# A two-layer hybrid block: instructions ordered by the scheduler's simulated timeline

## The chip, the cores and the metric

The program runs on one core of one Trainium2 chip. A core has a matrix engine (PE), a vector engine (DVE), a scalar engine (ACT), a general engine (POOL) and a queue engine (SP) that here only issues transfers. The engines share on-chip memory, run side by side and meet at semaphores. The metric is the device time of one execution in microseconds.

## What is computed

The reference is a backbone of two layers over 512 latent tokens and 256 context tokens, 1024 wide. One layer is, with the branches cut to their names:

```
h  = rmsnorm(x, g) * (1 + scale) + shift            # adaLN, scale/shift/gate from c
q, k, v, za, xr, zr, us, zs, gates = split(h @ w_in)
ya = diff_attention(q, k, v)    # 4 heads, two softmaxes each, head norm
yr = rglru(conv4(xr))           # both directions, block-diagonal gates
ys = glu(s5(us))                # both directions, complex diagonal states
m  = sum_n sigmoid(gates_n) * ((y_n * silu(z_n)) @ w_branch_n)
x  = x + gate * (m @ w_out)
```

Context tokens read context tokens only; latent tokens read all. The second layer needs no context output. A last norm gives the latent tokens.

## The kernel before

Tokens lie along the free axis, 512 latent and then 256 context, and channels on the 128 partitions. Each large product is three fp32r products (high by high, low by high, high by low), written by `product` (L180): per block of 128 input channels and per segment of tokens a 128x512 matmul and, where context is needed, a 128x256 one. `inproj` makes one tile `ps_in` of 128 output channels so, in 48 such matmuls (24 without context); `branch` makes `ps_b` in 24 (12). `wsplit` brings weights: SP loads `wr` (L161), ACT copies it to the high half `wh` (L162), and DVE forms the low half `wl` (L167); in a part of layer 0 a POOL transfer does instead.

A layer is written in this order. First the input of the S5 branch (`ps_us`). Then four LRUs, `lru(i)`: `ps_in`, a convolution on ACT and DVE (L822 to L827, tile `cv`), the split `uHL` (L830), four gate products `ps_g` of six matmuls each with an ACT function behind each (L840), then exponentials, a square root (L853) and three scans on DVE (L855, L858, L856, and a sum at L859). All tiles of the pool `lru` have one buffer: `cv` shares the place of `th`, which the sum at L859 reads last, and `uHL` that of `a2`. Between the LRUs stand the sixteen steps of the S5 scan (`ps_x`, `ps_y`), as many as a table `PLAN` says, and gate projections. Then come the LRU's output path, the S5's, and attention.

Attention (L1065 to L1118) goes head by head. For each block of 128 queries and each of two components, `ps_s` is a score block of four matmuls over 768 keys (two over 256 keys for the context queries); DVE takes its maximum (L1089, L1090) and ACT its exponential with the sum (L1091). The two components are put together on DVE (L1094 to L1097), transposed on PE (`ps_t`), split, and multiplied by the values (`ps_o`, L1113). After each head stand two output chunks of the S5 branch, each a gate projection `ps_in` and a `ps_b`. After the fourth head the squares of all heads are summed (`ps_ss`, L1128), a root is taken, and `ps_rr` (L1136) spreads it, one head at a time, to DVE (L1137).

The accumulator memory sets the pace: pool `acc` has two buffers of 1024 columns, `mis` two of 512 (`ps_t`, `ps_o`, `ps_x`, `ps_y`), and `big` **one** of 1024. `big` holds `ps_s`, `ps_g`, `ps_ss`, `ps_rr` in layer 0 and the queries' `ps_in` of every second head. So a score block starts only when ACT has read the block before. In layer 1 `big` becomes part of another pool after the LRUs.

The order of the instructions on each engine is not written by hand. The program text gives each instruction a place, which is its priority; a scheduler then walks through an imagined execution and, whenever an engine is free in it, issues the first instruction in program order whose operands and buffers are ready there. Each engine then keeps that order on the chip. Products of a later part of the program thus fill the gaps of a chain in an earlier part; they are called fill below. What counts as ready, and at which moment an engine is free, follows from the time that the scheduler has for each instruction.

## Time and profile before

| what | us |
|---|---|
| median of 3 runs | 1568.6 (1568.36 to 1571.8) |
| the profiled execution | 1571.89, of which the span is 1570.1 |
| PE busy with matmuls | 1489.2 (95%) |
| DVE busy | 1125.0 (72%) |
| ACT busy | 818.7 (52%) |
| POOL busy | 172.2 (11%) |

The profiled execution took 3.3 us more than the median. Times in the stretches named later count from the start of the span. The stages lie so in it: load, norm and S5 input of layer 0 up to 72 us; its LRUs and S5 scan to 355; S5 output and start of attention to 440; heads 0 and 1 to 574, heads 2 and 3 with the head norm to 720; merge, output projection and next norm to 935; S5 input of layer 1 to 990; its LRUs and S5 scan to 1137; outputs to 1250; attention to 1465; and the rest.

### The profile page before, as it was taken

What the parts mean: (1) busy time and instruction counts of PE and PEld (TensorE: products, weight loads), DVE (VectorE), ACT (ScalarE), POOL (GpSimd) and SP (SyncE); (2) the same over time, 40 slices, a digit from 0 to 9 for tenths busy, and PEclk for the clock granted to TensorE, in tenths of its full rate; (3) what the DMA queues carried; (4) which work ended last, traced back from release to release, by engine and by line L of the source; (5) the groups of instructions that cost most, each with busy time, mean ns of one, the idle gap of its engine ahead of it and who ended that gap; (6) DMA issues with size and microseconds to landing.
All of it is one profiled execution on the core that took longest, in us unless ns stands there. A gap on an engine that the chain in (4) does not pass through costs nothing. (4 is left out here: it accounts for less than half of the span.)

```text
span 1570.1 us, 24750 instructions
## 1 busy us (share of the span) xinstructions
PE 1489.2 (95%) x9096; PEld 1246.2 (79%) x9096; DVE 1125.0 (72%) x2312; ACT 818.7 (52%) x1468; POOL 172.2 (11%) x231
## 2 busy tenths in 40 slices
PE   4998899899999999999999999999999999999997
PEld 2786778788988888888778887777788988888777
DVE  6789899978367757658568863789775488397555
ACT  6676878664344534534325365666525365355433
POOL 1111111124000100000332310000000000000110
PEclk8998999999999999989999999999999999999999
DMA  8555444467311111115573762435454212111542
GB/s 279 167 151 119 112 110 105 89 158 197 94 52 43 42 53 46 49 34 177 193 250 125 258 201 82 143 111 162 118 168 132 81 61 58 65 61 54 174 148 94
DMA packets 111210, 189.13 MB, mean 120 GB/s; under 512 B 25328, under 2 KB 42352, under 8 KB 111088
## 3 DMA queue, kind: packets, MB, share of 16 engines
q1 hardware_dynamic: 97392, 158.17, 32.2%
q0 software_dynamic: 13696, 29.37, 8.1%
q8 instruction: 72, 1.18, 0.3%
q14 instruction: 50, 0.41, 0.1%
HBM read 145.02 MB, written 25.69 MB: 109 GB/s over the span
## 5 line engine op out<-in xcount | busy, mean ns | idle before, releaser
L162 ACT ACTIVATE wh<-wr 128x512 fp32r<-128x512 f32 x320 | 200.3, 629 | 367.2 <-PE ps_in L180 151.3
L180 PE MATMUL ps_in<-hH,wh 128*128 128x512 f32 x1248 | 376.5, 360 | 14.4 <-ACT wh L162 7.3
L180 PE MATMUL ps_in<-hH,wl 128*128 128x512 f32 x1248 | 378.6, 359 | 7.1 <-DMA wl<-wr 7.1
L180 PE MATMUL ps_in<-hL,wh 128*128 128x512 f32 x1248 | 375.5, 359 | 0.0
L167 DVE TENSOR_TENSOR wl<-wr,wh 128x512 fp32r<-128x512 f32 x264 | 187.5, 714 | 172.7 <-ACT wh L162 129.9
L180 PEld LDWEIGHTS ps_in<-hH,wh 128*128 128x128 f32 x1248 | 207.3, 192 | 52.3 <-ACT wh L162 8.4
L180 PEld LDWEIGHTS ps_in<-hH,wl 128*128 128x128 f32 x1248 | 207.7, 191 | 43.1 <-DMA wl<-wr 9.6
L180 PEld LDWEIGHTS ps_in<-hL,wh 128*128 128x128 f32 x1248 | 206.9, 191 | 31.8
L911 POOL TENSOR_TENSOR m<-m,g 128x768 f32<-128x768 f32 (+1 forms) x16 | 29.0, 1811 | 730.7 <-issue 348.4
L1091 ACT ACTIVATE p<-ps_s,mx 128x768 f32<-128x768 f32 (+1 forms) x80 | 65.2, 815 | 71.4 <-DVE mx L1090 67.5
L180 PE MATMUL ps_b<-yH,wh 128*128 128x512 f32 (+1 forms) x288 | 89.5, 359 | 0.6 <-DVE m L945 0.6
L180 PE MATMUL ps_b<-yL,wh 128*128 128x512 f32 (+1 forms) x288 | 88.0, 357 | 0.0
L180 PE MATMUL ps_b<-yH,wl 128*128 128x512 f32 (+1 forms) x288 | 87.7, 357 | 0.0
L1089 DVE TENSOR_REDUCE mx<-ps_s 128x1 f32<-128x768 f32 (+1 forms) x80 | 67.6, 847 | 23.9 <-PE ps_s L1086 23.3
L165 POOL DMA_DIRECT2D wl<-wr x56 | 49.0, 896 | 259.6 <-ACT wl L164 206.1
L180 PEld LDWEIGHTS ps_b<-yH,wh 128*128 128x128 f32 x288 | 48.2, 188 | 10.7 <-ACT wl L164 0.9
L180 PEld LDWEIGHTS ps_b<-yL,wh 128*128 128x128 f32 x288 | 47.7, 188 | 7.2
L180 PEld LDWEIGHTS ps_b<-yH,wl 128*128 128x128 f32 x288 | 47.6, 188 | 7.2
L180 PE MATMUL acc<-mH,wh 128*128 128x512 f32 (+1 forms) x160 | 49.2, 340 | 0.0
L180 PE MATMUL acc<-mH,wl 128*128 128x512 f32 (+1 forms) x160 | 48.8, 337 | 0.0
L180 PE MATMUL acc<-mL,wh 128*128 128x512 f32 (+1 forms) x160 | 48.8, 337 | 0.0
L1107 DVE TENSOR_TENSOR wTL<-ps_t,wTH 128x512 fp32r<-128x512 f32 (+1 forms) x72 | 35.9, 536 | 13.4 <-ACT wTH L1106 13.2
(357 smaller groups left out, 2901.1 us busy)
## 6 DMA issues: line engine op xcount, KB each, us to landing
wr<-in_win SPq DMA_DIRECT2D x208, 256.0 KB
wm<-in_wmod SPq DMA_DIRECT2D x48, 512.0 KB
wl<-wr POOLq DMA_DIRECT2D x56, 256.0 KB, 3.9
wr<-in_wbr SPq DMA_DIRECT2D x48, 256.0 KB
sp<-s5d SPq DMA_DIRECT2D x16, 768.0 KB
wr<-in_wout SPq DMA_DIRECT2D x32, 256.0 KB
s5d<-vv POOLq DMA_DIRECT2D x16, 320.0 KB, 3.2
usd<-up SPq DMA_DIRECT2D x8, 512.0 KB
```

The costliest lines, as they stand in the source:

```text
L162: S.activation(wh, raw, AF.Copy)
L165: G.dma_start(wl, raw, accum_op=OP.add)
L167: V.tensor_sub(wl, raw, f32(wh))
L180: PE.matmul(out[:, c0:c0 + n], lhsT=(wl if ps == 2 else wh)[:, k, :], rhs=rhs(k0 + k, ps == 1)[:, t0:t0 + n], start=st, stop=en)
L911: (V if n == 0 and dt >= ADD_V[l] else G).tensor_add(m_t[dt][:, :W], m_t[dt][:, :W], g[:, :W])
L1089: V.reduce_max(mx[:, 0:1], sc[:, :kw], axis=AX.X)
L1091: S.activation(p[c][:, :kw], sc[:, :kw], AF.Exp, bias=mx[:, 1:2], scale=0.125, accum_out=sm[:, c:c + 1])
L1107: V.tensor_sub(wTL[:, k0:k1, qi * 128:(qi + 1) * 128], src, f32(wTH[:, k0:k1, qi * 128:(qi + 1) * 128]))
```

## The change

One argument is added where the program is scheduled. The scheduler held a running sum of the durations of what it had issued to each engine, and took that for the time; now a simulation of the machine's timeline runs along with it and says what is done and which engine is free. No instruction of the computation is added or taken away: PE has the same matmuls, DVE, POOL and SP the same work, and ACT two loads of a function table fewer (34 for 36). Only their order on each engine differs, and with it the waits.

```diff
--- before.py
+++ after.py
@@ -1337,7 +1337,7 @@
         arrays[f"in_{name}"] = a[name]
         args.append(nc.dram_tensor(f"in_{name}", a[name].shape, F32, kind="ExternalInput").ap())
     args.append(nc.dram_tensor("out_T", (8, 128, T), F32, kind="ExternalOutput").ap())
-    with tile.TileContext(nc) as tc:
+    with tile.TileContext(nc, schedule_with_timeline_sim=True) as tc:
         hybrid_kernel(tc, *args)
     r = _run(nc, [arrays], core_ids=[0])
     o = np.asarray(r.results[0]["out_T"])
```

On PE the order differs over most of the program; it is alike at about 0 to 60 us, 360 to 440 and 1500 to 1560 us of the span of before. Three places follow. In the rows, a tile's name is followed by a running number.

The first is PE at the end of head 1 in layer 0. `ps_s` are the last score blocks, of context queries; `ps_v` is the values product of heads 2 and 3, and `ps_in_6127` the query projection of head 2, which takes the one buffer of `big`. Before:

```order
L1113 MATMUL ps_o_5663<-wTH_5585,vL_4562 128x256 x6
L1103 MATMUL ps_t_5707<-ident_105,p0_5685 128x128 x2
L1083 MATMUL ps_s_5715<-ks_5479,qs_5406 128x256
L1086 MATMUL ps_s_5715<-kL_4558,qs_5406 128x256
L1014 MATMUL ps_v_5941<-wh_5986,hL_325 128x256 x4
L1014 MATMUL ps_v_5942<-wh_5986,hL_325 128x256 x2
L1014 MATMUL ps_v_5941<-wl_5987,hH_324 128x256 x4
L1014 MATMUL ps_v_5942<-wl_5987,hH_324 128x256 x2
L1014 MATMUL ps_v_5941<-wh_6028,hH_359 128x256 x4
L1083 MATMUL ps_s_5722<-ks_5479,qs_5406 128x256
L1086 MATMUL ps_s_5722<-kL_4558,qs_5406 128x256
L1014 MATMUL ps_v_5942<-wh_6028,hH_359 128x256 x2
```

After:

```order
L1083 MATMUL ps_s_5695<-ks_5479,qs_5406 128x256
L1086 MATMUL ps_s_5695<-kL_4558,qs_5406 128x256
L1113 MATMUL ps_o_5663<-wTH_5585,vH_4561 128x256 x6
L1113 MATMUL ps_o_5663<-wTL_5586,vH_4561 128x256 x6
L1113 MATMUL ps_o_5663<-wTH_5585,vL_4562 128x256 x6
L1083 MATMUL ps_s_5715<-ks_5479,qs_5406 128x256
L1086 MATMUL ps_s_5715<-kL_4558,qs_5406 128x256
L1103 MATMUL ps_t_5707<-ident_105,p0_5685 128x128 x2
L1083 MATMUL ps_s_5722<-ks_5479,qs_5406 128x256
L1086 MATMUL ps_s_5722<-kL_4558,qs_5406 128x256
L180 MATMUL ps_in_6127<-hH_235,wh_6116 128x512
L180 MATMUL ps_in_6127<-hH_235,wh_6116 128x256
```

The rows of `ps_v` have gone from between the score blocks to a place ahead of them, and the query projection follows the last score block at once. The same holds ten score and transpose tiles back: between `ps_s_5539` and `ps_in_6127` no matmul of another part stands in the order of after. The end of head 3 looks alike there, from `ps_s_6977` to the third `ps_rr`.

The second is PE between the third and fourth LRU of layer 1. `ps_g_10982` is the last gate product of the third LRU, `ps_g_11303` the first one of the fourth, and `ps_in` are projections. Before:

```order
L180 MATMUL ps_g_10982<-uHL_10952,wl_10874 128x512
L180 MATMUL ps_g_10982<-uHL_10952,wl_10874 128x256
L180 MATMUL ps_in_11191<-hH_10005,wl_11187 128x512
L180 MATMUL ps_in_11191<-hH_10027,wh_11186 128x512
L180 MATMUL ps_in_11191<-hL_10028,wh_11186 128x512
L180 MATMUL ps_in_11191<-hH_10027,wl_11187 128x512
L180 MATMUL ps_in_11191<-hH_10031,wh_11186 128x512
L180 MATMUL ps_in_11191<-hL_10032,wh_11186 128x512
L180 MATMUL ps_in_11191<-hH_10031,wl_11187 128x512
L180 MATMUL ps_in_11235<-hH_9985,wl_11225 128x512
```

After:

```order
L180 MATMUL ps_g_10982<-uHL_10952,wh_10873 128x512
L180 MATMUL ps_g_10982<-uHL_10952,wh_10873 128x256
L180 MATMUL ps_g_10982<-uHL_10952,wl_10874 128x512
L180 MATMUL ps_g_10982<-uHL_10952,wl_10874 128x256
L180 MATMUL ps_g_11303<-uHL_11297,wh_11218 128x512
L180 MATMUL ps_g_11303<-uHL_11297,wh_11218 128x256
L180 MATMUL ps_g_11303<-uHL_11297,wh_11218 128x512
L180 MATMUL ps_g_11303<-uHL_11297,wh_11218 128x256
L180 MATMUL ps_g_11303<-uHL_11297,wl_11219 128x512
L180 MATMUL ps_g_11303<-uHL_11297,wl_11219 128x256
```

The projections that stood between the two LRUs, 16.33 us of PE's time there, have gone to an earlier place; from `ps_g_10974` to the fourth LRU's last gate product 36 gate matmuls stand in a row.

The third is PE at the norm ahead of layer 1. `ps_st` sums squares, `ps_rb` spreads the root, `ps_us` is the first product of layer 1, and `ps_w` and `acc` are output projections of layer 0. Before:

```order
L180 MATMUL ps_w_9824<-mH_9083,wh_9587 128x512
L215 MATMUL ps_rb_9803<-ident_105,rs_9800 128x128 x2
L180 MATMUL ps_w_9824<-mL_9084,wh_9587 128x512
L180 MATMUL ps_w_9824<-mH_9083,wl_9588 128x512
L180 MATMUL ps_w_9824<-mH_9087,wh_9593 128x512
```

After:

```order
L180 MATMUL acc_9878<-mH_9099,wh_9704 128x512
L207 MATMUL ps_st_9797<-ones_110,norm_0_9778 128x2 x2
L180 MATMUL acc_9878<-mL_9100,wh_9704 128x512
L180 MATMUL acc_9878<-mH_9099,wl_9705 128x512
L215 MATMUL ps_rb_9803<-ident_105,rs_9800 128x128 x2
L180 MATMUL ps_us_10060<-hH_9985,wh_9968 128x256
L180 MATMUL ps_us_10061<-hH_9985,wh_9974 128x256
```

The output projections that stood behind `ps_rb` now stand ahead of it, and the first product of layer 1 follows it directly.

## Rows read from the trace of the kernel before

**Rows 1.** The page: the span, and section 1, busy time, share and instructions.

```profile
span 1570.1 us, 24750 instructions
...
PE 1489.2 (95%) x9096; PEld 1246.2 (79%) x9096; DVE 1125.0 (72%) x2312; ACT 818.7 (52%) x1468; POOL 172.2 (11%) x231
```

**Rows 2.** Stages (us): length, busy (instructions) of PE, PEld, DVE, ACT, POOL; clock, DMA share, GB/s.

```profile
72.00:355.00 283.00, 260.29 (x1809) 218.04 (x1809) 251.56 (x556) 207.31 (x400) 41.79 (x49) 0.97 0.53 124
...
440.00:574.00 134.00, 131.94 (x826) 115.40 (x825) 87.06 (x169) 62.76 (x121) 8.14 (x4) 1.00 0.15 46
574.00:720.00 146.00, 144.25 (x848) 124.48 (x847) 96.34 (x181) 68.85 (x128) 7.37 (x4) 0.96 0.15 46
...
990.00:1137.00 147.00, 136.94 (x794) 111.69 (x791) 127.54 (x257) 91.72 (x122) 0.00 (x0) 0.97 0.43 129
...
1250.00:1465.00 215.00, 212.72 (x1185) 179.61 (x1184) 153.15 (x279) 110.70 (x204) 12.73 (x8) 0.99 0.20 61
```

**Rows 3.** Waits of PE in 72 to 355 us: total us, times, longest.

```profile
PE ps_in L180 <- ACT wh L162: 7.3, 3, 3.7
```

**Rows 4.** Order of time, a full score step: start us, us, engine, line, operation.

```profile
533.50 0.61 PE L1083 MATMUL ps_s<-ks,qs 128*128 128x512 f32 x2
...
534.90 0.95 DVE L1089 TENSOR_REDUCE mx<-ps_s 128x1 f32<-128x768 f32 x1
...
536.13 0.90 ACT L1091 ACTIVATE p<-ps_s,mx 128x768 f32<-128x768 f32 x1 [1.93 <-DVE mx L1090]
...
537.50 0.51 PE L1083 MATMUL ps_s<-ks,qs 128*128 128x512 f32 x2
```

**Rows 5.** Order of time, a context score step of the same head.

```profile
552.50 0.36 PE L1083 MATMUL ps_s<-ks,qs 128*128 128x256 f32 x1
...
554.88 0.39 PE L1083 MATMUL ps_s<-ks,qs 128*128 128x256 f32 x1
```

**Rows 6.** Four stretches, matmuls into ps_in alone; columns as in rows 2.

```profile
526.10:556.50 30.40, 4.65 (x25) 3.75 (x25) 0.00 (x0) 0.80 (x1) 1.00 0.15 45
671.40:718.00 46.60, 26.07 (x120) 20.34 (x121) 1.89 (x2) 1.61 (x2) 0.89 0.13 44
1069.90:1091.90 22.00, 16.33 (x79) 13.11 (x79) 0.00 (x0) 2.03 (x4) 1.00 0.42 130
1444.70:1467.40 22.70, 15.11 (x53) 9.97 (x53) 0.68 (x1) 0.58 (x1) 0.92 0.18 54
```

**Rows 7.** Two of these stretches, matmuls into ps_b alone.

```profile
526.10:556.50 30.40, 5.33 (x24) 3.67 (x24) 0.94 (x1) 1.00 0.15 45
671.40:718.00 46.60, 3.65 (x17) 2.52 (x17) 0.94 (x1) 0.89 0.13 44
```

**Rows 8.** The first of these stretches, matmuls into ps_v alone.

```profile
526.10:556.50 30.40, 11.14 (x87) 10.81 (x88) 0.00 (x0) 0.00 (x0) 1.00 0.15 45
```

**Rows 9.** Order of time, first and third broadcast of the head norms.

```profile
712.23 0.82 PE L1136 MATMUL ps_rr<-ident,rs 128*128 128x128 f32 x6
...
717.07 0.82 PE L1136 MATMUL ps_rr<-ident,rs 128*128 128x128 f32 x6
```

**Rows 10.** Order of time, third LRU of layer 1 to the fourth's input.

```profile
1070.37 0.89 ACT L840 ACTIVATE gi<-ps_g,prm 128x768 f32<-128x768 f32 x1
...
1084.61 0.68 DVE L859 TENSOR_TENSOR ysum<-ysum,th 128x512 f32<-128x512 f32 x1
...
1090.46 0.84 ACT L830 ACTIVATE uHL<-u 128x768 fp32r<-128x768 f32 x1 [0.88 <-DVE u L827]
```

**Rows 11.** Order of time, the norm ahead of layer 1.

```profile
920.43 0.58 PE L207 MATMUL ps_st<-ones,norm 128*128 128x2 f32 x4 [1.35 <-DVE norm L202]
...
922.07 0.42 DVE L225 TENSOR_TENSOR xn<-xn,ps_rb 128x256 f32<-128x256 f32 x1 [0.56 <-PE ps_rb L215]
```

**Rows 12.** Two stretches near the end of layer 0's attention; columns as in rows 2.

```profile
697.80:708.00 10.20, 10.20 (x42) 9.43 (x42) 1.03 (x2) 2.05 (x5) 0.00 (x0) 0.50 0.08 27
708.00:718.00 10.00, 10.00 (x70) 9.09 (x69) 5.88 (x8) 6.12 (x8) 0.00 (x0) 1.00 0.24 79
```

## The prediction

> **What bounds the kernel now.** I read the page first: PE is busy 1489.2 of 1570.1 us [rows 1]. At most 81 us of its idle time can be won by any order, and since the set of matmuls stays the same, that is the whole prize. Next I cut the span into stages to see where the idle time lies [rows 2]. In 440 to 574 us PE is busy 131.94 of 134 us, in 574 to 720 144.25 of 146, in 1250 to 1465 212.72 of 215. These attention stages are full; another order can leave them alone or open holes in them. Idle time of size stands in the two LRU and S5 stages: 283 less 260.29 is 22.7 us in layer 0, 147 less 136.94 is 10.1 us in layer 1. DVE is the second engine there, busy 251.56 of 283 and 127.54 of 147 us [rows 2], so these stages are shared between PE and DVE. Of the 22.7 us, 7.3 are three waits of a projection for the weights that ACT copies [rows 3]; the rest is many small waits. So the prize is about 33 us in two places, and the risk is everywhere else.
>
> What keeps the attention stages full is fill. A full score step, four matmuls, DVE maximum, ACT exponential, then the next block, runs from 533.50 to 537.50, 4.00 us [rows 4]; DVE's 0.95 us and ACT's 0.90 us in it are time in which PE can't touch the next score block, since `big` has one buffer. A context step goes from 552.50 to 554.88, 2.38 us [rows 5]. PE's own part of a full step is two pairs of matmuls such as the one of 0.61 us [rows 4], about 1 us. Before, other products stand between. For the 30.4 us from 526.1 to 556.5 they are 4.65 us of `ps_in` [rows 6], 5.33 of `ps_b` [rows 7] and 11.14 of `ps_v` [rows 8], 21.1 us together; the chain's own products take the other 9.3.
>
> **The change part by part.** The order rows show one pattern in most stages. The new order puts more fill between chain steps early in a head, so that the fill is used up before the chain ends; the last steps then stand back to back. Early in the head this costs nothing, since PE does the fill anyway. At the end PE meets a score block whose buffer isn't free, and behind it nothing but more of the same chain, and it stands. I take from the trace, and show in the row pairs, that PE executes its matmuls in the order given, so what has gone ahead can't come back.
>
> *End of head 1, layer 0.* From `ps_s_5539` to the next query projection no fill is left. The chain is five full steps and four context steps: 5 x 4.00 + 4 x 2.38 = 29.5 us [rows 4, 5]. The query projection needs `big`, so it can't pass. PE's own products in the stretch are 9.3 us, so it stands up to 20 us. The measured steps had fill queued ahead of their score blocks; with none, a full step can't be under the matmuls plus 0.95 plus 0.90 and some hand-overs, for which I estimate 3.4 us, a context step 2.0, together 25 and a stand of 15.7. I take **+17** (15 to 20).
>
> *End of head 3, layer 0.* From 671.4 to 718.0 us before, 46.6 us hold 26.07 us of `ps_in` [rows 6] and 3.65 of `ps_b` [rows 7]; none of it stands there now, and 16.9 us of own work and waits remain. The chain is the rest of one full step (3.3 estimated), three full and four context steps (12.0 and 9.5), then the last transposes, values, squares and root (some 5, estimated from operations of this size), and the broadcasts, which take 4.8 us from the first to the third start since one buffer carries them [rows 9]: 34.6 us. Less 16.9 that is 17.7; with the short steps 13. I take **+16** (12 to 20; the ceiling is the fill, 29.7).
>
> *End of layer 1's attention.* The stretch 1444.7 to 1467.4 holds 15.11 us of `ps_in` [rows 6], of which the order after leaves almost none. The first two places lose 17 of 21.1 and 16 of 29.7 us of fill, 0.54 to 0.81 of it. That gives 8 to 12; here score blocks have more than one buffer, so I take the lower end, **+8** (3 to 13). Head 1 of layer 1 loses a microsecond at most; I leave it out.
>
> *Norm ahead of layer 1.* `ps_rb` before has output projections behind it, and now the first product of layer 1, which needs the normed stream. In the trace the sums start at 920.43, the first normed chunk is made on DVE from 922.07 for 0.42 us [rows 11], and ACT and two splits follow before a matmul can start, and eight chunks come one by one. I take **+5** (1 to 10). I exclude a gain, because the projections that moved ahead stand where PE is full already.
>
> *LRUs of layer 1.* Between the third and the fourth LRU the order had 16.33 us of projections [rows 6], and now the gate products follow each other. They can't run so: the third's functions start at 1070.37, its last sum is made at 1084.61 (only then is the fourth's `cv` free), and the fourth's split starts at 1090.46 [rows 10]. PE would stand for about 20 us less what S5 products remain there. The moved 16.33 us of projections can fill idle time earlier in the stage, but of that there were only 10.1 us, and part of it is DVE's doing. The last LRU, too, finishes with less ahead of the output path. From 0, if the moved fill closes all holes, to 28, if both ends stand, I take **+15**.
>
> *LRUs and S5 of layer 0.* Here the change may win. Counted as the matmuls that stand ahead in the order, each at its spacing in the trace, projections come some 5 to 15 us of PE work earlier, gate products and S5's products later. The stage's last S5 product stands about 22 us of PE work later than before, but the stage ends with the first product of the S5 output, at the same place on PE, and DVE's work ahead of it is nearly the same. The ceiling is the 22.7 us of idle time [rows 2]; DVE's own 31 us of idle time (283 less 251.56) bounds it from the other side. The waits for ACT's weight copies, 7.3 us [rows 3], are what earlier projections can win. I take **-8** (-16 to +8).
>
> *Clock.* In 697.8 to 708.0 us the granted clock is 0.50, its lower level, and 42 matmuls run where the next 10 us carry 70 [rows 12]: about 4 us lost. New stands may bring another such stretch, and moved ones may take one away: **+3** (-4 to +10). By the Trainium skill, page "TensorE: Matmul & The Clock Gate", section "HAM oscillation — how this bites in real kernels", waits of PE between bursts throttle the array, and the next burst starts cold. This case's row speaks against it as the only cause: PE was busy 10.20 of 10.20 us in the slow stretch [rows 12]. By that rule each of the five stands would bring about one such loss and the sum would be some 17 us higher.
>
> *Nothing else moves on the path.* DVE, ACT, POOL and SP carry the same work; the weight transfers that SP issues move with the projections they feed, three buffers ahead at most, and the attention stages use 0.15 of the transfer engines [rows 2], so they have room. Two table loads fewer lie on ACT, which has slack.
>
> Sum: 17 + 16 + 8 + 5 + 15 - 8 + 3 = **+56** us. Against the profiled execution's 1571.9 that is 1628; it stood 3.3 us above the median, so by the median of 1568.6 it is **1625 us**.
>
> **The rivals.**
> - *Half of it.* The chains run faster without fill in their way than I count, and the moved projections close layer 1's holes: 8 + 8 + 4 + 3 + 0 - 8 + 3 = +18, 1587 us. For it speaks that steps were measured with fill between; against it that DVE and ACT rows alone make most of a step.
> - *Slower through layer 0.* S5's scan starves DVE because its PE products come up to 34 us of PE work later, and the stage grows by 12 where I take -8: +76, 1645 us. It decides when DVE is idle for more than the 31 us of before in that stage.
> - *The clock follows every stand*, by the rows' price of 4 us each for five stands in place of 3 in all: +73, 1642 us.
> - *Faster.* The fill goes early because it really closes holes there, in both LRU stages (-16 and -10), and the tails cost little, because the chains in the middle of a head, relieved, run ahead of what I assume: tails 4 + 4 + 2 + 2, so -14, 1555 us. It decides if PE's busy share stays above 0.97 from 526 us to the end of layer 0's attention. Against it: in the order, the chain in the middle of a head is not relieved, it comes 20 to 39 us of PE work later.
> - *No effect.* PE carries 1489.2 us whatever the order, and the order differs only where engines wait anyway: 1569 us.
>
> **How the numbers follow.** Forecast 0.53; half 0.18; layer 0 slower 0.08; clock 0.10; faster 0.08; no effect 0.03. The range takes in the half case and the two slower ones: 1584 to 1650; outside it lie the faster case, no effect and the far ends of the unknown costs, about 2 in 10. A change under 0.2%, some 3 us, can't be told from none here. Faster by more than that 0.08, within it 0.04, slower 0.88.
>
> **What would show it.** In the trace of after: PE waits for ACT's exponential (L1091) in a row of score blocks at the end of heads 1 and 3, 4 us apart and near 15 us of idle time each; `ps_in_6127` at the end of the first; PE waiting for `uHL` some 15 to 20 us between the third and fourth LRU of layer 1; a first stage to the S5 output that is shorter by some 8 us. I am wrong if PE's busy share in the attention of layer 0 is as high as before, or if the idle time of the LRU stages falls by more than the attention loses.

## The result, and the profile after

The changed kernel takes 1678.9 us in the median of four runs (1677.7 to 1681.2), the kernel before, on the same chip, 1570.2 us. The ratio is 1.069, with an interval of 1.067 to 1.072. The sign was forecast, the size was not: the sum gave +56 us and the range ended at 1650; the measured change is +109 us.

The page of after, its span and its busy times, answers to [rows 1]:

```profile
span 1676.2 us, 24789 instructions
...
PE 1522.1 (91%) x9096; PEld 1284.2 (77%) x9096; DVE 1131.5 (68%) x2312; ACT 811.0 (48%) x1466; POOL 176.4 (11%) x231
```

PE carries the same 9096 matmuls. The span grew by 106.1 us: PE is busy 32.9 us longer and idle 73.2 us longer. The mean granted clock fell from 0.982 to 0.938, and PE's busy time grew with it: stretches at the lower level (1.2 GHz) cover 210 us after and 58.5 before. Half of PE's busy time in them is what the lower level cost the matmuls: about 45 us more than before.

Here is the time by stage. A stage goes from the first matmul of one tile to the first matmul of another, the same two tiles in both traces. "Clock" is what the lower level cost more than before, half of PE's busy time in its stretches; it is a part of the change of busy time, which other things lower too. Cells left empty lie between -1.7 and +2.9.

| stage | before | after | change | PE idle | clock |
|---|---|---|---|---|---|
| start, first product of layer 0 | 81.4 | 87.7 | +6.3 | +5.2 | |
| LRUs and S5, layer 0 | 273.9 | 277.9 | +4.0 | +6.2 | |
| outputs of it | 89.0 | 88.1 | -0.9 | | |
| heads 0 and 1, layer 0 | 129.1 | 148.8 | +19.7 | +15.7 | +7.1 |
| heads 2 and 3, layer 0 | 189.3 | 211.3 | +22.0 | +11.9 | +13.3 |
| outputs and norm | 174.4 | 177.2 | +2.8 | | |
| first product of layer 1 | 29.1 | 40.8 | +11.7 | +4.4 | +6.7 |
| LRUs of layer 1 | 160.7 | 191.6 | +30.9 | +20.8 | +6.3 |
| outputs of it | 133.5 | 131.6 | -1.9 | | |
| attention, layer 1 | 211.2 | 220.7 | +9.5 | +7.0 | +4.3 |
| end | 98.5 | 100.4 | +1.9 | | |

The same places as windows of after, in the columns of [rows 2] (length, busy time of PE, PEld, DVE, ACT, POOL with instructions, granted clock, DMA share, GB/s):

```profile
77.00:365.00 288.00, 258.28 (x1810) 220.67 (x1808) 242.37 (x519) 204.40 (x397) 40.63 (x47) 0.94 0.53 122
...
454.00:600.00 146.00, 130.69 (x796) 116.34 (x794) 87.28 (x167) 59.14 (x117) 8.89 (x4) 0.93 0.14 40
600.00:780.00 180.00, 163.11 (x911) 143.41 (x912) 99.58 (x183) 70.67 (x133) 9.30 (x4) 0.88 0.18 55
...
986.00:1056.00 70.00, 59.03 (x315) 49.83 (x314) 28.06 (x57) 37.61 (x67) 1.34 (x3) 0.88 0.39 130
1056.00:1235.00 179.00, 148.16 (x855) 122.53 (x855) 136.32 (x283) 91.52 (x121) 0.00 (x0) 0.87 0.37 115
```

The two attention stages of layer 0 were 98.5 and 98.8 per cent full in [rows 2]; now PE is busy 130.69 of 146 and 163.11 of 180 us. In the layer-1 LRUs it stands for 30.8 of 179 us. DVE has the same operations as before (2312, busy 1131.5 us for 1125.0 in all), so what holds PE is not a fuller engine but an order in which engines wait for each other.

The waits of PE in after, at the end of head 1 (545 to 605 us: total us, times, longest):

```profile
PE ps_s L1083 <- ACT p L1091: 8.0, 4, 2.9
```

and in the layer-1 LRUs from 1140 to 1235 us:

```profile
PE ps_g L180 <- ACT uHL L830: 18.5, 1, 18.5
PE ps_y L665 <- DVE st L646: 5.7, 1, 5.7
```

Both were named ahead: score blocks that wait for the exponential, and a stand of 15 to 20 us ahead of the fourth LRU's gates. The stand is there; what it is worth is another matter, since it is not where the stage lost its time.

**The LRUs of layer 1.** The input of each LRU is split by one ACT operation, L830. Its four starts clock the stage. Before:

```profile
992.33 0.84 ACT L830 ACTIVATE uHL<-u 128x768 fp32r<-128x768 f32 x1 [1.42 <-DVE u L827]
...
1025.87 0.85 ACT L830 ACTIVATE uHL<-u 128x768 fp32r<-128x768 f32 x1 [1.59 <-DVE u L827]
...
1057.37 0.84 ACT L830 ACTIVATE uHL<-u 128x768 fp32r<-128x768 f32 x1
...
1090.46 0.84 ACT L830 ACTIVATE uHL<-u 128x768 fp32r<-128x768 f32 x1 [0.88 <-DVE u L827]
```

After:

```profile
1058.27 0.85 ACT L830 ACTIVATE uHL<-u 128x768 fp32r<-128x768 f32 x1 [0.85 <-DVE u L827]
...
1102.69 0.84 ACT L830 ACTIVATE uHL<-u 128x768 fp32r<-128x768 f32 x1 [4.35 <-DVE u L827]
...
1149.95 0.84 ACT L830 ACTIVATE uHL<-u 128x768 fp32r<-128x768 f32 x1
...
1186.33 0.84 ACT L830 ACTIVATE uHL<-u 128x768 fp32r<-128x768 f32 x1 [3.33 <-DVE u L827]
```

Before, the steps are 33.5, 31.5 and 33.1 us; after, 44.4, 47.3 and 36.4. Together they grew by 30.0 us, which is the stage's loss. The step with the 18.5 us stand grew by 3.3 us only. The other 26.7 us were lost in the first two steps, in which PE is hardly idle, as the windows of after show over these steps and over the third:

```profile
1058.00:1150.00 92.00, 90.43 (x569) 75.83 (x569) 76.97 (x170) 49.31 (x70) 0.00 (x0) 1.00 0.45 142
1150.00:1187.00 37.00, 17.73 (x98) 14.45 (x94) 24.48 (x45) 18.30 (x23) 0.00 (x0) 0.79 0.35 105
```

In the first two the projections that had moved ahead stand between the gate products of one LRU. The second LRU's gates run from 1104.00 to 1126.65 us, 22.7 us; before, they ran from 1027.24 to 1037.38, 10.1 us. The matmuls into `ps_in` alone in these two stretches, after and then before:

```profile
1104.00:1126.65 22.65, 14.57 (x63) 11.21 (x64) 0.00 (x0) 1.97 (x4) 1.00 0.69 217
```

```profile
1027.24:1037.38 10.14, 5.55 (x21) 3.74 (x22) 0.00 (x0) 0.60 (x1) 1.00 0.37 127
```

Products of the S5 scan stand there too, 4.8 us for 0.6. The first LRU's gates take 17.9 us for 11.9. So 18.5 of the 26.7 us lie inside the two LRUs' gates; the rest lies behind them, on the way to the next input. An LRU's gates, its functions on ACT and DVE, and the next LRU's input are one serial chain. Fill in its middle delays all that follows, and the stand at its end is what is left of the fill that went ahead.

**Attention of layer 0.** The same reading holds. The first matmul pair of full score blocks in after, head 0:

```profile
463.44 0.52 PE L1083 MATMUL ps_s<-ks,qs 128*128 128x512 f32 x2
...
503.47 0.52 PE L1083 MATMUL ps_s<-ks,qs 128*128 128x512 f32 x2
```

and in before:

```profile
450.19 0.62 PE L1083 MATMUL ps_s<-ks,qs 128*128 128x512 f32 x2 [0.19 <-ACT ks L1057]
...
478.51 0.52 PE L1083 MATMUL ps_s<-ks,qs 128*128 128x512 f32 x2
```

Six steps lie between the rows in each: 40.0 us after, 28.3 before, with 26.5 us of projections among them for 12.4. The end of head 1 in after:

```profile
555.75 0.51 PE L1083 MATMUL ps_s<-ks,qs 128*128 128x512 f32 x2
559.52 0.62 PE L1083 MATMUL ps_s<-ks,qs 128*128 128x512 f32 x2 [2.92 <-ACT p L1091]
...
575.70 0.58 PE L1083 MATMUL ps_s<-ks,qs 128*128 128x256 f32 x1 [2.32 <-ACT p L1091]
...
586.05 0.39 PE L1083 MATMUL ps_s<-ks,qs 128*128 128x256 f32 x1 [1.08 <-ACT p L1091]
```

Five full steps take 19.95 us, 3.99 each, as the 4.00 of [rows 4]. From the first of these blocks to the last it is 30.3 us, and in before, with 21 us of fill between, 29.4 (from 525.48 to the 554.88 of [rows 5]). So at the end of a head the pace is that of the maximum and the exponential, with fill or without. The stage's 19.7 us had been lost before 555 us, when the chain came late: from the stage's first matmul to the block at 555.75 it is 102.1 us, before 81.2. PE's idle time at the end is where the loss shows.

### The profile page after: what moved, and what is told of

The parts are those of the page before. It is cut to its first block, busy times and chain, and to the rows that moved or that the text cites. A ratio compares the mean times of both kernels' runs of the same rounds, so it can differ in the third digit from the quotient of the medians.

```text
span 1676.2 us, 24789 instructions
## 1 busy us (share of the span) xinstructions
PE 1522.1 (91%) x9096; PEld 1284.2 (77%) x9096; DVE 1131.5 (68%) x2312; ACT 811.0 (48%) x1466; POOL 176.4 (11%) x231
## 5 line engine op out<-in xcount | busy, mean ns | idle before, releaser
L180 PE MATMUL ps_in<-hH,wh 128*128 128x512 f32 x1248 | 374.4, 358 | 11.9 <-DVE vL L1022 3.7
L180 PE MATMUL ps_in<-hH,wl 128*128 128x512 f32 x1248 | 373.9, 357 | 2.1 <-DMA wl<-wr 2.1
L180 PEld LDWEIGHTS ps_in<-hH,wl 128*128 128x128 f32 x1248 | 206.2, 191 | 36.4 <-DMA wl<-wr 3.4
L911 POOL TENSOR_TENSOR m<-m,g 128x768 f32<-128x768 f32 (+1 forms) x16 | 31.8, 1985 | 862.8 <-DVE g L910 836.2
L180 PE MATMUL ps_b<-yL,wh 128*128 128x512 f32 (+1 forms) x288 | 87.7, 358 | 0.5 <-DVE yL L879 0.5
L180 PE MATMUL ps_g<-uHL,wh 128*128 128x512 f32 (+1 forms) x128 | 34.5, 384 | 25.3 <-ACT uHL L830 19.5
L1083 PE MATMUL ps_s<-ks,qs 128*128 128x256 f32 (+1 forms) x144 | 41.2, 359 | 14.8 <-ACT p L1091 14.8
L180 PEld LDWEIGHTS ps_b<-yL,wh 128*128 128x128 f32 x288 | 47.7, 189 | 8.4 <-DVE yL L879 0.8
L180 PEld LDWEIGHTS ps_b<-yH,wl 128*128 128x128 f32 x288 | 47.7, 188 | 8.0
L180 PE MATMUL acc<-mH,wh 128*128 128x512 f32 (+1 forms) x160 | 49.4, 341 | 0.0
```

The lines of the kernel that those rows point to most:

```text
L180: PE.matmul(out[:, c0:c0 + n], lhsT=(wl if ps == 2 else wh)[:, k, :], rhs=rhs(k0 + k, ps == 1)[:, t0:t0 + n], start=st, stop=en)
L911: (V if n == 0 and dt >= ADD_V[l] else G).tensor_add(m_t[dt][:, :W], m_t[dt][:, :W], g[:, :W])
L1083: PE.matmul(sc[:, c0:c0 + w], lhsT=qs[:, c, qt * 128:(qt + 1) * 128], rhs=kk[:, c, t0:t0 + w], start=True, stop=False)
```

## The experiments

Most of them tie the order of engines, or of a stretch, to that of one kernel or the other. A tie is an edge between two instructions of one engine that makes the scheduler keep them in that order and adds no wait in the program. All share one edit; the table holds runs of instruction numbers (first+count), and its first row stands with each experiment (in 5 to 7 and 12 the numbers are those in the instructions' names). The engines that are not tied are ordered anew around those that are, so in these runs their order is neither kernel's. How far it lies from each is given as the number of operations that would have to move to give that kernel's order, by their names and shapes in the traces; between before and after that is 790 of DVE's 2312 operations and 2677 of PE's 9096 matmuls. The edit:

```diff
-    mis_st.close()
+    mis_st.close(); pin(tc)
...
+def pin(tc):
+    eng = mybir.EngineType.PE
+    seen = [i for i in tc.nc.cur_bb.bb.instructions if i.engine == eng and i.opcode == "Matmult" and i.name not in EXTRA]
...
+        for x, y in zip(order, order[1:]):
+            tc.add_manual_dep(seen[y], seen[x].name, info, reason="order")
```

**1. The changed kernel, all of PE in the order of before.**

```diff
+PINS = [(
+    "0+36 68+2 74+2 80 36+2 70+4 38+2 76+4 81+7 92 40+4 88+3 44+2 91 93+4 46+2 97+7 48+2 104+5 50+2 109+10 52+8 "
...
```

> The changed kernel (simulated timeline orders the program), but PE's matmuls are tied, by edges that set order alone, to the order of the kernel before, over the whole program. DVE, ACT, POOL and SP stay with the new scheduler. Theory A (PE's order carries the loss: fill used up ahead of the ends of the chains): the loss of 108 us goes, 1570 to 1590 us. Rival B (the order on DVE, ACT and the queues carries it: splits and chain steps issued late there): at least half of the loss stays, over 1625 us.

1629.5 us, ratio 1.038 (1.035 to 1.041). PE's order by itself isn't the change: more than half of the loss stays when PE has its old order back. What stays is the loss of a third order: 562 of DVE's operations would have to move to give the order of before, 620 to give that of after. By stage: attention of layer 0 +9.6 us in place of +41.7, so PE's order carried most of it there; but layer 0's LRUs +12.7, layer 1's LRUs +14.4 and layer 1's attention +17.4, the last more than in after itself.

**2. The kernel before, all of PE in the order of after.**

```diff
+PINS = [(
+    "0+6 12+8 6+6 20+16 68+2 74+2 80+2 36+10 70+4 76+4 82+4 46+2 86+2 92+2 98+2 48+2 88+4 94+4 100+4 50+2 104+2 "
...
```

> The mirror of the first: the scheduler of before (running sum of durations) on DVE, ACT, POOL and SP, PE tied to the order of the changed kernel over the whole program. Theory A: the whole loss comes, 1665 to 1690 us. Rival B: under 1625 us.

1746.4 us, ratio 1.112 (1.109 to 1.115): slower than after itself, by 67 us. The other engines did not keep the old order; the old scheduler placed them around the tied PE, on DVE 669 operations away from before and 492 from after. PE's order alone does not set the time: with this order of the others it costs 67 us more than with that of after. This ended the theory with which I began, that PE's order alone carries the change.

**3. The kernel before, PE in the order of after in the layer-1 LRUs alone.**

```diff
+PINS = [(
+    "5444+19 5360+2 5463 5424 5464+2 5362+4 5466+11 5425+8 5366+6 5433+5 5477+11 5438+6 5372+6 5488+25 5378+6 5513+3 "
...
```

> The kernel before, with PE tied to the order of after in the LRU and S5 stage of layer 1 alone (845 matmuls from ps_g_10378 on). The change's trace loses 30 us there, the prediction had 15. Theory A: 25 to 35 us more than before, about 1600 us, with one wait of PE of some 18 us for the fourth LRU's split. Rival B: under 10 us. If the 30 us came from the stage being entered late rather than from the order in it, under 15 us.

1608.3 us, ratio 1.025 (1.022 to 1.028), +39 us; the stage grew by 43.2 us. L830 in this kernel:

```profile
990.13 0.84 ACT L830 ACTIVATE uHL<-u 128x768 fp32r<-128x768 f32 x1 [1.42 <-DVE u L827]
...
1039.50 0.84 ACT L830 ACTIVATE uHL<-u 128x768 fp32r<-128x768 f32 x1
...
1087.16 0.84 ACT L830 ACTIVATE uHL<-u 128x768 fp32r<-128x768 f32 x1 [1.68 <-DVE u L827]
...
1129.95 0.84 ACT L830 ACTIVATE uHL<-u 128x768 fp32r<-128x768 f32 x1 [3.33 <-DVE u L827]
```

The steps are 49.4, 47.7 and 42.8 us. The placement of the projections on PE is enough to stretch the LRU chain, in every step. DVE and ACT had to follow it in the stage (104 and 57 operations away from before), which may be a part of the 43.2 us.

**4. The changed kernel with the 18.5 us stand filled.** 68 matmuls whose result is overwritten keep PE busy ahead of the fourth LRU's gates; the rest of PE is tied to after's own order.

```diff
-                    a = 2 * d + ax
+                    a = 2 * d + ax; warm(PE, pg, hH, l, i, a)
...
+    for _ in range(68 if (l, i, a) == (1, 3, 0) else 0):
+        r = PE.matmul(pg[:, :T], lhsT=hH[0][:, :128], rhs=hH[1][:, :T], start=True, stop=True)
```

> The changed kernel with its own PE order and 68 more matmuls of 128x512 (their result is overwritten) just ahead of the fourth LRU's gate products in layer 1, where PE stood 18.5 us and then ran 47.8 us at the lower clock (1171 to 1219 us). They fill about 15 us of the stand. Theory C (the clock falls because PE stands, and this costs time of its own behind the stand): the low stretch goes or shrinks to under 17 us, and the time falls 8 to 15 us against the changed kernel, to 1664 to 1671 us. Rival D (the stage behind the stand is set by ACT and DVE, so the clock costs nothing): within 3 us of 1679. If the matmuls delay the chain, the time grows.

The stand in this kernel, and the first gate product behind it:

```profile
1166.61 17.20 PE L1417 MATMUL ps_g<-hH 128*128 128x512 f32 x68 [2.07 <-ACT gi L840]
1183.65 1.03 PE L180 MATMUL ps_g<-uHL,wh 128*128 128x512 f32 x4
```

and in after:

```profile
1187.22 2.00 PE L180 MATMUL ps_g<-uHL,wh 128*128 128x512 f32 x4 [18.50 <-ACT uHL L830]
```

The four matmuls ran at the higher level, 1.03 us in place of 2.00, and the time at the lower level there fell from 47.8 us (1171.2 to 1219.0) to 27.3. The stage fell from 191.6 to 190.0 us, and the whole took 1675.1 us, ratio 1.068 (1.066 to 1.070), an interval that overlaps that of after. So 20 us less at the lower level gave back 1.6 us at most: here the chain goes over ACT and DVE. The filling itself held the gates up by some 0.6 us, since their input was done at 1183.01.

**5. The changed kernel, PE, DVE and ACT in the order of before; SP and POOL left to the new scheduler.**

```diff
+PINS = [(
+    "156+6 166+6 212+4 218+4 225+2 242+4 248+4 255+2 271+2 275+2 574+2 580+2 586+2 592+2 277+2 578+2 584+2 590+2 "
...
+), (
+    "53 111 113+2 173+4 181 101+2 141 143 145 148 150 152 462 154 463 501+2 464 503 417 431 418 465 419 164 504 420 "
...
```

> The changed kernel with PE, DVE and ACT tied to the order of before; SP's and POOL's issue order is the new scheduler's. With PE alone tied (the first experiment) 60 us of loss remained. Theory A2 (the order of the chain's steps on DVE and ACT, which the new scheduler set for a PE that it sees stand, carries the rest): 1565 to 1585 us. Rival E (the weight transfers' order on SP and POOL carries it): at least 30 us of the 60 stay, 1600 us and more. If the edges themselves cost time, it also stays above 1585.

1588.6 us, ratio 1.012 (1.008 to 1.015): +18 us are left with the order of SP and POOL alone. It is not that of after: 84 of SP's 679 transfers are away from before and 114 from after, and 4 of POOL's 231 operations from before. So the order of transfers can cost 18 us at equal work; what it costs in after isn't shown. The 18 us are in layer 0's LRUs (+5.4), in the outputs and norm behind attention (+6.2) and in layer 1's LRUs (+3.3). One wait of PE from 780 to 930 us shows how, at the weights of layer 1's S5:

```profile
PE ps_st L485 <- ACT strip L498: 6.3, 3, 5.8
```

In before the same wait is 0.8 us in three times. I did not test it by itself.

**6 and 7. The same with PE and DVE, and with PE and ACT, in the order of before.** The edit of 5 without the table of ACT in run 6, as shown, and without that of DVE in run 7.

```diff
-), (
-    "51 100 139+2 142 144 146+2 149 151 153 416 163 195 201 207 436 453 232 429 223 430 454 233+2 253 237 262+2 449 "
...
```

> PE and DVE tied to the order of before, ACT left to the new scheduler. If DVE's order carries the remaining 60 us: 1570 to 1590 us. If ACT's (weight copies ahead of exponentials, score chain late): 1610 us and more. If either alone leaves a mismatch: between.

1601.9 us, ratio 1.020 (1.016 to 1.024).

> PE and ACT tied to the order of before, DVE left to the new scheduler; the counterpart of the run before. If ACT's order carries the 60 us: 1570 to 1590. If DVE's: 1610 and more.

1654.4 us, ratio 1.053 (1.050 to 1.057). With PE's order restored, restoring DVE's as well gives 28 us, restoring ACT's as well costs 25, the rest being ordered anew each time. The loss at the start of the kernel (+7.4 us in run 1) is gone with DVE restored (+0.4).

**8. The changed kernel with late attention of layer 0 kept busy**: six overwritten matmuls ahead of each group of transpositions in heads 1 and 3, the rest of PE tied to after's own order.

```diff
-                        pt = mis("ps_t")
+                        pt = mis("ps_t"); warm(PE, pt, hH, l, h, q0)
...
+    for _ in range(6 if l == 0 and h in (1, 3) and q0 > 0 else 0):
```

> The changed kernel with its own PE order and, in the last two thirds of heads 1 and 3 of layer 0, six more 128x512 matmuls ahead of each transposition group (48 and 24 of... their result is overwritten), about 1.4 us each group, in places where PE waited 1.5 to 2.9 us for the score chain. In the changed kernel these two ends ran 21.8 and 46.4 us at the lower clock, and matmuls at that clock cost 7.1 and 13.3 us more than at the higher. Theory C2 (there the lower clock is on the path, since PE, DVE and ACT take turns in the chain): the low stretches shrink by half or more and the time falls 6 to 15 us against 1679. Rival D2 (as in layer 1's LRUs, the clock is not on the path, or the added matmuls delay the chain as much): within 4 us of 1679, or longer.

1678.9 us, ratio 1.069 (1.065 to 1.072), no change from after. Windows at the ends of heads 1 and 3, after:

```profile
555.00:605.00 50.00, 32.22 (x156) 27.16 (x155) 26.85 (x59) 17.50 (x39) 0.00 (x0) 0.76 0.05 16
735.00:790.00 55.00, 40.58 (x183) 35.07 (x182) 27.22 (x63) 18.56 (x36) 0.00 (x0) 0.63 0.17 53
```

and with the filling:

```profile
555.00:605.00 50.00, 37.58 (x204) 32.27 (x202) 25.43 (x58) 17.22 (x39) 0.00 (x0) 0.89 0.06 18
735.00:790.00 55.00, 44.46 (x232) 38.84 (x231) 28.09 (x65) 19.79 (x39) 0.00 (x0) 0.78 0.16 56
```

The clock is higher (0.89 for 0.76, 0.78 for 0.63), the stages are 149.6 and 209.5 us long for 148.8 and 211.3. The lower level lies mostly beside the path here. The filling takes PE time too and might hide a gain, but only where PE had no idle time left.

**9. The kernel before, PE in the order of after in layer 0's LRUs alone.**

```diff
+PINS = [(
+    "398+5 342+14 403+19 470+5 356+4 475+8 314+2 483+6 316+4 489+8 360+8 497+2 368+2 320+6 370+4 499+7 422+6 506+5 "
...
```

> The kernel before, with PE tied to the order of after in the LRU and S5 stage of layer 0 alone (1334 matmuls from ps_x_1079 on). The prediction put -8 us on this stage, the changed kernel lost 4.0 us in it. Theory F (the projections that moved ahead delay the LRU and S5 chains as in layer 1, and no idle time is won): 3 to 20 us slower than before, 1573 to 1590. The prediction's step (earlier projections win the waits for ACT's copies): 1555 to 1567 us.

1602.2 us, ratio 1.022 (1.020 to 1.024); the stage +25.0 us, the next +4.1. PE's waits in this stage of the run:

```profile
PE ps_wt L529 <- DVE wt L522: 8.8, 2, 6.0
PE ps_in L180 <- DMA wl<-wr: 7.3, 2, 4.2
```

The first is new, and the second was 5.2 us in four times before. The gain of 8 us forecast here does not come in this order, around which DVE and ACT were placed anew (175 and 207 operations away from before). In after itself, with other orders of DVE and ACT, the stage lost 4.0 us.

**10. The same for the norm ahead of layer 1 and its first product.**

```diff
+PINS = [(
+    "4670+29 4654+6 4699+13 4728+14 4660+4 4712+2 4742+9 4714+4 4751 4664+6 4752+6 4718+4 4758+18 4780+48 4838+5 "
...
```

> The kernel before, with PE tied to the order of after in the output projection of layer 0, the norm and the first product of layer 1 alone (563 matmuls from ps_st5_9014 on). The prediction had 5 us for it, the changed kernel lost 11.7 us in the first product, of which 4.4 are idle time and 6.7 the price of the lower clock. If the order of these products is the cause and the clock is on the path, since PE here is fed product by product: 9 to 14 us slower, about 1581. If the clock is not on the path: 4 to 6 us. If the loss came from what stood before the stage: under 2 us.

1584.8 us, ratio 1.010 (1.008 to 1.012), +16.6 us: +4.7 in the stage that ends with the norm, +11.4 in the product, as the +11.7 in after. So PE's order is enough for the loss in this place (56 operations of DVE and 33 of ACT followed it), and in run 1, with that order taken back, the product took about 2 us less than before.

**11. The same for heads 0 and 1 of layer 0.**

```diff
+PINS = [(
+    "2369+24 2228+4 2393+33 2232+4 2426+34 2242+4 2460+10 2236+6 2470+19 2246+4 2489+33 2274+4 2522+13 2250+6 "
...
```

> The kernel before, with PE tied to the order of after in heads 0 and 1 of layer 0 alone (765 matmuls from ps_s_4900 on). The changed kernel lost 19.7 us there, the prediction had 17. Theory G (fill placed between the early score blocks delays the chain, and the chain's end takes the same 30 us whether fill stands in it or not): 16 to 24 us slower, 1586 to 1594, and the stretch from the start of ps_s_5539 to that of ps_s_5722 again 29 to 31 us. If the order on DVE and ACT made the loss: under 8 us.

1593.3 us, ratio 1.016 (1.015 to 1.018), +25 us, +20.8 of them in the stage, as the +19.7 in after. From the block at 542.99 to the last at 574.77 it took 31.8 us, near the 29.4 of before: again the loss had come ahead of the tail.

**12. The changed kernel, DVE and ACT in the order of before; PE, SP and POOL left to the new scheduler.**

```diff
+PINS = [(
+    "53 111 113+2 173+4 181 101+2 141 143 145 148 150 152 462 154 463 501+2 464 503 417 431 418 465 419 164 504 420 "
...
```

> The changed kernel with DVE and ACT tied to the order of before; PE, SP and POOL left to the new scheduler, which then places PE's fill around that. PE alone tied to before took 50 us of the 108 away (first experiment). Theory H (orders belong together: PE's place for the fill and DVE's for the chain's steps each carry about half): 1610 to 1660 us. Rival I (PE's order alone is the cause, DVE's only follows): 1665 us and more, since PE's fill again goes early. Rival J (DVE's and ACT's order is the cause): under 1600 us.

1824.8 us, ratio 1.163 (1.160 to 1.167), the slowest of all. That is in the range of "1665 us and more", but not for its reason, the fill of after, since PE does not have the order of after here: 2540 of its matmuls would have to move to give that, and 2267 to give that of before. The largest wait of PE in it, over the whole span:

```profile
PE ps_s L1083 <- ACT p L1091: 40.3, 20, 2.9
```

In after:

```profile
PE ps_s L1083 <- ACT p L1091: 14.8, 9, 2.9
```

The orders of the engines belong together. Tied to one kernel's order on some engines and ordered anew on the rest, a program can be slower than both kernels (runs 2 and 12), so the parts that the transplants give (34, 25, 17 and 39 us in runs 9, 11, 10 and 3) are not parts of one sum; they make 115 us without two of the attention places.

**13. Run 10 with the stand ahead of the first product filled** by 14 overwritten matmuls.

```diff
-        pus = [acc("ps_us"), acc("ps_us"), big("ps_us")]
+        pus = [acc("ps_us"), acc("ps_us"), big("ps_us")]; warm(PE, pus[0], wus[0][0][0], l)
...
+    for _ in range(14 if l else 0):
```

> The kernel before with TensorE tied to the changed kernel's order in the first product of layer 1 (as in the run that took 1584.8 us), and 14 overwritten 128x512 matmuls behind the last reduction of that norm, in the stand in front of the product, so that its first matmuls need not run at the lower clock (in the run without them the low stretches are 932.6 to 942.9 and 953.1 to 963.3 us, 20.5 us, and the matmuls of the stage cost 5.5 us more than before). Theory L, the lower clock is on the path here, since the product keeps TensorE busy: the low time falls by 8 to 20 us and the stage by 2.5 to 5.5 us, the whole to 1579 to 1582 us. Theory M, the clock is not on the path here either: the low time falls and the stage stays within 1.5 us, the whole 1583 to 1587 us. If the low time does not fall, neither is tested.

1580.8 us, ratio 1.007 (1.005 to 1.009). The windows of the product, run 10 and then this one:

```profile
932.00:968.00 36.00, 23.23 (x118) 20.66 (x119) 19.51 (x40) 21.32 (x43) 0.00 (x0) 0.72 0.27 97
```

```profile
932.00:968.00 36.00, 24.07 (x128) 21.03 (x127) 20.00 (x42) 21.80 (x44) 0.00 (x0) 0.81 0.29 103
```

The time at the lower level fell from 20.5 to 13.6 us, less than the first theory asked for, and the product's own matmuls took 29.8 us for 31.1; the stage shortened by 0.8 us, 40.55 to 39.75. That fits the theory that PE is on the path here, but it is too small to decide it. The time of the whole, 1580.8 for 1584.8, is not from this stage: 2.2 us of it are in the LRUs behind, where a fall of the clock at 1004.3 us did not come. Not settled.

## Why the prediction was wrong, point by point

**The mechanism** was right in part: fill that is placed early leaves stands at the ends of chains. The stands came at the places named and with the releasers named. What failed is "Early in the head this costs nothing, since PE does the fill anyway", and its like for the LRUs: the chain pays for fill where the fill is put, and the stand at the end shows it. Three terms were too small, and one had the wrong sign.

- *Layer-1 LRUs, +15 forecast, +30.9 measured*: the largest miss. The step that failed is "The moved 16.33 us of projections can fill idle time earlier in the stage". They stand in the first two steps, where PE had 3.8 us of idle time before (61.25 of 65.04 us busy from 992.33 to 1057.37) and the stage grew by 26.7; they split the gate products of the first two LRUs and delayed the chain (run 3 and the starts of L830). I priced the gap between the third and the fourth LRU, 3.3 us of the loss, and left out the delay of the two before, 26.7 us.
- *Layer-0 LRUs, -8 forecast, +4.0 measured*, and +6.3 at the start, which I had not priced. The step that failed is "The waits for ACT's weight copies, 7.3 us [rows 3], are what earlier projections can win". In after these waits are indeed gone, but others came, at the weights of the S5 scan (77 to 365 us; 0.3 us before):

```profile
PE ps_wt L529 <- DVE wt L522: 5.7, 1, 5.7
PE ps_wt L529 <- DVE strip L500: 3.7, 1, 3.7
```

  A win in one wait was counted as a win on the path. Run 9, with 25 us lost, points the same way, but in an order of DVE and ACT that after does not have.
- *Norm, +5 forecast, +11.7 measured*, outside its bounds of 1 to 10; run 10 gives +11.4 with PE tied in this stretch alone. The eight chunks were named but not counted. In after PE waits there, from 985 to 1035 us, for

```profile
PE ps_us L180 <- ACT hH L739: 7.3, 3, 3.5
PE ps_us L180 <- DVE hL L740: 2.6, 1, 2.6
```

  and its matmuls cost 6.7 us more at the lower clock, of which it is not settled how much is on the path (run 13).
- *Head 3, +16 forecast, +22.0 and +2.8 behind it*. The mis-sized piece is "the last transposes, values, squares and root (some 5, estimated from operations of this size)". In after, from the last score to the first broadcast:

```profile
755.96 0.39 PE L1083 MATMUL ps_s<-ks,qs 128*128 128x256 f32 x1 [0.99 <-ACT p L1091]
757.76 4.95 PE L1128 MATMUL ps_ss<-ones,sqo 128*128 128x2 f32 x24 [1.30 <-ACT p L1091]
...
771.85 1.54 PE L1136 MATMUL ps_rr<-ident,rs 128*128 128x128 f32 x6 [0.71 <-DVE rs L1131]
```

  it is 15.9 us, for which the sum has 7.4 (these 5 and a context step). The three context steps ahead of it took 3.6 us each for 2.38. Part of the miss is hidden by a slip: behind 671.4 us the trace of before has two more full blocks, at 674.66 and 679.03, where the sum counts three steps, 4 us too many. The trace of before had the same piece with fill in it, from a last score at 693.03 to the 712.23 of [rows 9], 19.2 us. It could have been read in place of estimated.
- *Head 1, +17 forecast, +19.7 measured*, inside its bounds; run 11 gives +20.8. The full step estimated at 3.4 us took 3.99, as the row of before said, and a context step 3.45 on the mean (575.70 to 586.05) for the 2.0 estimated. The number holds, but the time was lost ahead of the end (20.9 us), and the end took 30.3 us for 29.4.
- *Layer-1 attention, +8 forecast, +9.5 measured*: the number is right, the reason isn't shown. No run ties this stage by itself, and run 1 shows +17.4 there with PE's order restored.
- *Clock, +3 forecast*. The lower level came much more often (210 us for 58.5), and its price hangs on the place. In the stands and the ends of chains it was low: runs 4 and 8 took 20 and 27 us of it away; the one gained 1.6 us in its stage, the other 1.0 us in two stages and nothing in the whole. Where PE is full it is on the path. Heads 2 and 3 of layer 0 have the same order on PE, DVE and ACT in before, run 10 and run 13, and 10.2, 6.8 and 3.4 us at the lower level; they took 189.4, 187.9 and 186.6 us. The windows of before and of run 13:

```profile
573.36:762.75 189.39, 186.90 (x1115) 158.91 (x1113) 132.97 (x262) 82.88 (x153) 13.15 (x11) 0.97 0.24 78
```

```profile
572.22:758.79 186.57, 184.19 (x1114) 156.07 (x1113) 133.05 (x262) 82.92 (x153) 13.17 (x11) 0.99 0.24 79
```

  PE's busy time falls by 2.7 us and the stage by 2.8, so the prediction's price of about 4 us for 10.2 fits there. The Trainium skill, page "TensorE: Matmul & The Clock Gate", section "HAM oscillation — how this bites in real kernels", says that waits between bursts throttle the array and the next burst starts cold. This case agrees on that: the stand from 1168.7 us is followed by gates at half speed. It doesn't follow that the time lost by the matmuls is lost to the kernel. The rival "the clock follows every stand" named the right event at a price that holds where PE is full and mostly lies beside the path in these stands.
- *"Nothing else moves on the path"*: wrong. With PE, DVE and ACT in their old order, another order of SP's transfers cost 18 us (run 5), and with PE alone restored another order of the rest cost 60 us (run 1). I looked at PE's order and took equal work on the others for equal time.

Of the rivals, "slower through layer 0" came nearest in size (+76 for +109) and had the wrong place; "faster" and "no effect" are out; "half of it" rested on moved fill closing layer 1's holes, and PE's idle time in that stage grew from 10.1 to 30.9 us. The terms as measured add up to 106.0 us, the growth of the span. What remains open is how the loss divides between engines: no run holds the other engines to the order of after while PE changes, so the ties don't divide it.

## What to carry to other kernels

When an order moves fill, follow the serial chain through the whole stage, by the starts of one operation that recurs in it, and price how late each step comes, not the gap at its end. Fill moved into a chain that has no slack costs its own length there and comes back as idle time at the end, where it is easily taken for the cause. Compare the order on every engine, those that issue transfers too. And when one engine is tied to another order, look at what the scheduler did with the rest: the time is that of a new schedule, which can be slower than both.

## What the runs showed of the hardware that I had not expected

Kept busy through the stand, PE still fell to the lower level soon after: in run 4 the windows over the filled stand and behind it read

```profile
1166.00:1190.00 24.00, 20.80 (x86) 16.62 (x86) 13.54 (x12) 11.70 (x11) 0.00 (x0) 0.93 0.00 1
1190.00:1214.00 24.00, 16.20 (x88) 13.45 (x87) 19.36 (x36) 12.17 (x14) 0.00 (x0) 0.51 0.27 83
```

The level fell at 1190.3 us, behind gates with waits of 1.0 and 1.6 us for ACT. In the second window PE was busy 16.20 of 24 us, with two more waits of 1.0 us and one of 5.7 us for DVE, and the granted clock was 0.51. In after, the level that fell in the 18.5 us stand stayed low until 1219.0 us, 31.8 us past the first gate at 1187.22. It stayed low through gates with waits of 1.0 us and through S5 products with a 5.7 us stand among them. Run 4, in which that stage met 20 us less of it, gained 1.6 us there: the waits for ACT and DVE set the pace.
